# Layer-0 attention scores in four pieces of 260 columns, two to a pair of PSUM banks

## The chip, the cores and the metric

The kernel runs on one core of a Trainium2 chip. The metric is the device time of one execution in microseconds (us); the median of three runs stands for the kernel. TensorE (PE) multiplies and writes into PSUM, eight banks of 128 partitions x 512 float32 columns. VectorE (DVE), ScalarE (ACT) and GpSimd (POOL) work on 128 partitions at a time; DVE and ACT read PSUM, POOL works on SBUF alone here. Each engine takes its own instructions in order and waits on semaphores for the others.

## The reference

The program is an encoder trunk of two layers over 16 meta tokens and 1024 real ones, 1040 in all, with 1024 features. Each layer is `h + mixer(rmsnorm(h))` and then `h + mlp(rmsnorm(h))` with a squared ReLU; a final norm follows. The part that is changed is the mixer of layer 0, two groups of attention heads side by side:

```python
# A: 4 heads, each with two softmaxes over all 1040 keys
s = einsum('bqhcd,bshcd->bhcqs', q, k) * scale + bias      # c = 0, 1
p = softmax(s)
out_a = rmsnorm((p[c=0] - lam * p[c=1]) @ v) * (1 - lam_init)
# B: 8 query heads in two groups that share keys and values, no bias
out_b = softmax(einsum('bqkgd,bskd->bkgqs', q, k) * scale) @ v
h = h + concat(out_a, out_b) @ w_out
```

## The kernel before

Activations lie transposed, features on partitions and tokens along the free axis. A float32 product is made of passes over exact high and low parts.

The attention of layer 0 works on query tiles of 128 tokens. The unit of the first half of the work is a *job*: one query tile against one set of keys, which `scores` turns into the unnormalized probabilities of a [128, 1040] tile `sp` (`s` in the code). For A, head by head, a query tile has two jobs (c = 0, 1), and each head has one more small job for the 16 meta queries: 4 x (8 x 2 + 1) = 68 jobs. For B, `attend_b` takes two query tiles, each one job; with a small job for the meta queries of each group there are 66. That is 134 jobs.

`scores` cuts the 1040 keys into three chunks of 348, 346 and 346 columns (`CH_ALL`). For a chunk PE makes two matmuls (the high and the low part of the keys) into one PSUM bank of the ring "sc" (L500, L502). DVE takes the bank out into `s`, with the bias added in A (L504) or as it is in B (L507), and the same instruction accumulates the row minimum into a column of `mx`. After the three chunks DVE reduces the three columns to one (L514), and ACT makes the exponential of all 1040 columns in place and sums it (L516):

```python
mn = sm.tile([P, 2], F32, tag="mn", name=nm("mn"))
V.tensor_reduce(mn[:M, :n_], mx[:M, :n_], op=ALU.min, axis=AX.X)
A.activation(s[:M, :L], s[:M, :L], AF.Exp, bias=mn[:M, x:x + 1], scale=-1.0, accum_out=sums[:M, x:x + 1])
```

In A, POOL then combines the two probability tiles of a query tile (`head_a`: a scaling, L619, and an addition, L620; both over 1040 columns in SBUF); in B, POOL scales each by its inverse sum (`attend_b`, L673). The second half, `pv`, is a generator that is queued up to three groups behind (`AHEAD`): PE transposes the probabilities into a bank of the ring "tr" (L543), ACT takes out the high part `ph` (L557), DVE the low part `plo` (L559), and PE multiplies by the values into a bank of the ring "pv" (L572). At the end of a group ACT copies that bank out in A (L626); in B ACT copies half of it (L680) and DVE adds the other half to it (L686). After each head of A a norm follows: small DVE operations on [128, 9] tiles (`rsqrt_small`, L159 to L164; also L636).

PSUM is shared out by tags: `BANKS` gives the tags a, b, c two banks each and d, e one; `RINGS` says in which order a use goes around its tags: "sc" over c, c, d (three banks), "tr" over a, a, e (three), "pv" over b, b (two). One PSUM pool serves the whole kernel, so the projections before and the dense phases after use the same banks.

The program text sets what depends on what; a planner in the framework sets the order of the instructions on each engine, by its own cost figures, and places the semaphores.

Of the kernel before, what the change touches and what calls it, by code (L numbers as in the profile page):

```python
"""Two-layer encoder trunk (differential + axial GQA mixer, windowed GQA mixer, squared-ReLU MLPs).

Activations are held transposed, [feature, token], tokens in their own order (16 meta, 1024 real).
float32 products run as float32r passes over exact high/low parts of both operands.
"""
# [16 lines left out]
P = 128  # L22
L = 1040
# [23 lines left out]
BANKS = {"a": 2, "b": 2, "c": 2, "d": 1, "e": 1}  # L47
RINGS = {"proj": "ccde", "nat": "aa", "back": "bb", "sc": "ccd", "tr": "aae", "pv": "bb",
         "mm": "aaeccd", "st": "aaeccdbb", "sm": "bb", "pj1": "d", "pj1_first": "dcc", "sc1": "cc"}
WR = 2  # L50
# [24 lines left out]
def trunk(tc, hT, gT, w_in0, w_out0, w_up, w_down, w_in1, w_out1, rel, sinks, lamv, subln, qkn,  # L75
# [13 lines left out]
    def lay_out(pl, tags):  # L89
        """fix where a pool's slots lie: a first tile of each tag, in this order, handed to its first users."""  # L90
        kept = {}
        for tag, shape, dt, bufs in tags:
            kept[tag] = [pl.tile(shape, dt, tag=tag, bufs=bufs, name=nm(tag))]

        def get(tag, shape, dt, bufs):
            if kept.get(tag):
                return kept[tag].pop()
            return pl.tile(shape, dt, tag=tag, bufs=bufs, name=nm(tag))

        return get  # L100
# [6 lines left out]
    psU = pool("banks", space=PSUM)  # L107
    at, sqp = {}, []

    def bank(ring):  # L110
        i = at.get(ring, 0)
        at[ring] = i + 1
        tag = RINGS[ring][i % len(RINGS[ring])]
        return psU.tile([P, 512], F32, tag=tag, bufs=BANKS[tag], name=nm(ring))

# [22 lines left out]
    def load_w(src, lo_on=V, parts=1, to=None):  # L138
        """a [128, 8 x 128] tile of weights as the split halves of its columns."""
        raw = wp.tile([P, 1024], F32, tag="wr", bufs=WR, name=nm("wr"))  # L140
        for i in range(parts):
            c = slice(1024 // parts * i, 1024 // parts * (i + 1))
            D.dma_start(raw[:, c], src[:, c])
        return [split_w(raw[:, 512 * i:512 * i + 512], lo_on, to and to[i]) for i in range(2)]

    def mm3(ps, w, xh, xl, o, n, k0=0, k1=KT):
        """ps[:, :n] = the product over k from k0 to k1 (added to what is there if k0 > 0), columns o to o + n."""
        for k in range(k0, k1):
            wh, wl = w[k // 4]
            for i, (a, x) in enumerate(((wh, xh), (wh, xl), (wl, xh))):  # L150
                T.matmul(ps[:, :n], a[:, k % 4 * P:(k % 4 + 1) * P], x[k][:, o:o + n],  # L151
                         start=(k == 0 and i == 0), stop=(k == len(xh) - 1 and i == 2))

    def rsqrt_small(x, pw, n):
        """1/sqrt(x) of a [pw, n] tile by three Newton steps from the shifted-exponent guess."""
# [27 lines left out]
    def colsum(acc, c0, n, ps, scale, eps=None):  # L183
        """rows of mean(acc over partitions)+eps, one column for each token tile, then 1/sqrt."""
# [20 lines left out]
    def bcast_cols(y, tiles, newps, use):  # L205
        """use(psum, first column, width) gets y's entries laid along the free axis on every partition."""
# [10 lines left out]
    def make_r(acc, c0, n, smps, newps):  # L217
        """1/rms of the columns, over the sums of squares; acc may itself be wider."""
        y, tiles = colsum(acc, c0, n, smps, 1.0 / 1024)
        r = acc  # L220
        bcast_cols(y, tiles, newps, lambda ps, o, w: A.copy(r[:, o:o + w], ps[:, :w]))
        return r

# [41 lines left out]
    def project0(m, scale=None, w=None, raw=False, tags=()):  # L265
        """[128 columns of the projection, tokens] of the normed input; raw: without the norm's factor yet."""
# [15 lines left out]
    def spill_pair(i, parts):  # L282
        """high and low parts of [128, tokens] to DRAM; parts: [(source, first column, width)]."""
# [8 lines left out]
    def natural(z, use):  # L292
        """transposes of [128, tokens] by token tiles, four to a bank."""
# [16 lines left out]
    # axial rotary tables times the norm's gain  # L310
# [17 lines left out]
    def rope(z, tab, fscale, i_out):  # L328
        """normalize and rotate a pair of heads [2 x 64, tokens]."""
# [62 lines left out]
    # relative-position bias vectors, negated, to DRAM  # L392
# [5 lines left out]
    # each copied to 128 rows: read back with a row pitch shorter by one, row p is shifted by p  # L398
# [19 lines left out]
    # lambda  # L418
# [57 lines left out]
    def advance():  # L476
        """one piece of the oldest late work."""
# [9 lines left out]
    def beside(n, keep):  # L487
        """n pieces of late work, as long as more than keep works are waiting."""
# [4 lines left out]
    def scores(jobs, M, sums):  # L493
        """exp(q k + bias - row maximum) for each job, its row sums in the columns of sums.
        jobs: [([(q, k)], probabilities, bias)]; the products come out negated."""
        n_ = len(jobs)
        mx = sm.tile([P, 2, 3], F32, tag="mx", name=nm("mx"))
        for c, (o, n) in enumerate(CH_ALL):
            for x, (ops, s, bias) in enumerate(jobs):
                ps = bank("sc")  # L500
                for i, (q, k) in enumerate(ops):
                    T.matmul(ps[:M, :n], q, k[:, o:o + n], start=(i == 0), stop=(i == len(ops) - 1))  # L502
                if bias is not None:
                    V.tensor_tensor_reduce(out=s[:M, o:o + n], in0=ps[:M, :n], in1=bias[:M, o:o + n], scale=1.0,  # L504
                                           scalar=mx[:M, x, c - 1:c] if CHAIN and c else BIG, op0=ALU.add, op1=ALU.min, accum_out=mx[:M, x, c:c + 1])
                else:
                    V.tensor_scalar(s[:M, o:o + n], ps[:M, :n], 1.0, None, op0=ALU.mult, op1=ALU.min,  # L507
                                    accum_out=mx[:M, x, c:c + 1])
                beside(BESIDE, AHEAD - 1)
        if CHAIN and bias is not None:  # L510
            mn = mx[:, :, 2]
        else:
            mn = sm.tile([P, 2], F32, tag="mn", name=nm("mn"))
            V.tensor_reduce(mn[:M, :n_], mx[:M, :n_], op=ALU.min, axis=AX.X)  # L514
        for x, (_, s, _) in enumerate(jobs):
            A.activation(s[:M, :L], s[:M, :L], AF.Exp, bias=mn[:M, x:x + 1], scale=-1.0, accum_out=sums[:M, x:x + 1])  # L516
# [6 lines left out]
    def pv(ps_o, ptiles, vmats, passes, lo_pool=()):  # L523
        """ps_o[:, columns of the query tiles] = sum over keys; ptiles: [(probabilities, rows)]."""
# [10 lines left out]
        def split(r):  # L535
            run = runs[r]
            kw = TW[run[0]]
            pt = bank("tr")
# [41 lines left out]
    def head_a(h):  # L580
# [18 lines left out]
        for grp in GRPS:  # L599
            ptiles = []  # L600
            for t in grp:
# [13 lines left out]
                # p0 - lambda p1, each row times the sum of its first softmax: the norm after it takes that out  # L615
# [6 lines left out]
            def values(grp=grp, ptiles=ptiles):  # L622
                po = bank("pv")
# [7 lines left out]
        def norm_a():  # L631
# [5 lines left out]
            y, tiles = colsum(osq, 0, L, bank("tr"), 1.0 / 128, e0)  # L637
# [4 lines left out]
            def norm_b():  # L642
                yield
                bcast_cols(y, tiles, lambda: bank("tr"), fin)
# [17 lines left out]
    def attend_b(g, ptq, store):  # L662
# [12 lines left out]
        def values():  # L675
            po = bank("pv")
# [31 lines left out]
    run_late(0)  # L708
    pA.release()
    pE.release()  # L710
    if stop == "mix0":
# [6 lines left out]
        psU.release()  # L718
# [12 lines left out]
    def dense(layer, chunks, halves, sub, w_out, h_src, xp, yp, st, ht, by_pool, late_k,  # L731
              finish, done, last, spare=None, extra=None):
        """ht += mix w_out, then the feed-forward block added to ht.
        The feed-forward products run as seven half-size block products in place of eight (Winograd's form of
        Strassen's identity, over halves of k, rows and tokens); all of the hidden layer goes to DRAM between the
        two. The last 512 hidden features are taken directly, by groups of token chunks, their weights kept in tiles
        from spare() or loaded for each group."""
# [181 lines left out]
        # the pairs that the second products start with come last, and stay  # L919
# [15 lines left out]
        def after(n, e=0):  # L935
            """queue behind the n-th of the last part's additions (e=0) or sums of weights (e=1)."""
# [3 lines left out]
        def blocks(k, r1, r2, th, tl, n):  # L940
            """the seven token-side factors of tiles k of both halves of this part."""
# [149 lines left out]
    def split_q(src, q0, q1):  # L1091
        """[two heads x 64, n] to the stacks [high; low] and [low; high]."""
# [12 lines left out]
    def project1(w, z, o, n, ring, c, scale=1.0):  # L1105
        """columns o to o + n of a projection, to z from column c."""
# [15 lines left out]
    # keys: [meta, 0, 1, meta, 2, 3, meta, 4, 5, meta, 6, 7, meta] along the free axis  # L1122
# [160 lines left out]
    psU.release()  # L1283
# [24 lines left out]
def _layout(np, x, meta_tokens, rel_table, norm_attn, norm_mlp, norm_final, w_in_even, w_out_even, diff_lambda,  # L1308
# [4 lines left out]
    def second(w):  # L1313
        """by 512 rows: the four blocks of (tiles of rows in turn, halves of columns); the last 512 rows by pairs of column tiles."""
# [43 lines left out]
```

## Time and profile before

| | |
|---|---|
| median of three runs | 2626.34 us (2625.93 to 2629.81) |
| span of the profiled execution | 2630.9 us |
| share of the span busy: PE, DVE, ACT, POOL | 95%, 74%, 48%, 49% |
| scores of A, first to last | 254 to 465 us of the span |
| scores of B, first to last | 465 to 686 us |
| last products with the values of B | 725 us |

The profile records one execution. An instruction's row gives its start from the begin of the span and its duration; a duration includes waiting inside the instruction and the filling of the engine's pipeline, so the next row can start before the one ahead has ended. A busy share of PE counts such overlapped durations and does not mean that PE is at its peak. The idle time before an instruction is put down to the instruction that released it, as far as the semaphores show.

### The profile page before, as it was taken

How to read it: one execution, taken by the hardware profiler on the slowest of the kernel's cores; microseconds unless marked ns; L12 is line 12 of the kernel's file. 1: busy time of each engine (PE TensorE's matmuls, PEld its weight loads, DVE VectorE, ACT ScalarE, POOL GpSimd, SP SyncE). 2: the span in 40 equal slices, each digit the busy share in tenths (PEclk: the TensorE clock that was granted, in tenths of full speed). 3: DMA queues.
4: the chain of work that ended last, by engine and by line, in shares of the span. 5: the costliest groups of instructions: out<-in, count | busy, mean ns of one | idle time of the engine just before them, and what ended most of it. 6: DMA issues, size and time to landing. Idle time of an engine off the chain costs nothing. (4 is left out here: it accounts for less than half of the span.)

```text
span 2630.9 us, 42960 instructions
## 1 busy us (share of the span) xinstructions
PE 2508.9 (95%) x15440; PEld 2233.5 (85%) x15440; DVE 1937.8 (74%) x4057; ACT 1265.7 (48%) x2562; POOL 1281.2 (49%) x1214
## 2 busy tenths in 40 slices
PE   7999999999998999989999999999989999899997
PEld 7999888888898899988999988887868888676776
DVE  7834887798748566689898757777575656989975
ACT  3322656677634344453433547777344444443434
POOL 3300765333145223268877344556453223889854
PEclk9999999999998999999999999999989999999998
DMA  4378433200131532323232342232312332233322
GB/s 133 117 243 260 111 95 93 49 11 11 67 123 42 173 114 98 114 82 105 82 106 90 117 120 71 65 88 61 121 44 101 112 112 96 96 96 98 102 75 80
DMA packets 105494, 261.09 MB, mean 99 GB/s; under 512 B 16864, under 2 KB 48320, under 8 KB 104768
## 3 DMA queue, kind: packets, MB, share of 16 engines
q1 hardware_dynamic: 105280, 258.35, 30.9%
q8 instruction: 121, 1.98, 0.3%
q14 instruction: 93, 0.76, 0.1%
HBM read 191.40 MB, written 75.40 MB: 101 GB/s over the span
## 5 line engine op out<-in xcount | busy, mean ns | idle before, releaser
L854 PE MATMUL st<-h,wh 128*128 128x260 f32 (+1 forms) x2520 | 811.9, 326 | 45.3 <-DVE h L998 14.5
L854 PE MATMUL st<-l,wh 128*128 128x260 f32 (+1 forms) x2520 | 810.2, 324 | 6.6 <-DVE l L779 4.0
L854 PE MATMUL st<-h,wl 128*128 128x260 f32 (+1 forms) x2520 | 782.9, 325 | 14.8 <-DVE wl L135 8.8
L854 PEld LDWEIGHTS st<-h,wh 128*128 128x128 f32 x2520 | 480.3, 191 | 98.9 <-DVE h L998 19.9
L854 PEld LDWEIGHTS st<-h,wl 128*128 128x128 f32 x2520 | 474.4, 191 | 63.0 <-POOL wl L135 12.8
L854 PEld LDWEIGHTS st<-l,wh 128*128 128x128 f32 x2520 | 481.8, 191 | 45.0 <-DVE l L779 4.6
L134 ACT CAST wh<-wr 128x512 fp32r<-128x512 f32 x378 | 233.3, 619 | 408.7 <-PE st L854 228.7
L135 DVE TENSOR_TENSOR wl<-wr,wh 128x512 fp32r<-128x512 f32 x254 | 215.0, 848 | 178.9 <-ACT wh L134 178.3
L864 POOL TENSOR_TENSOR ws<-wr 128x512 f32<-128x512 f32 x32 | 43.2, 1350 | 412.7 <-DMA wr<-w_up 332.1
L135 POOL TENSOR_TENSOR wl<-wr,wh 128x512 fp32r<-128x512 f32 x124 | 177.0, 1430 | 67.0 <-ACT wh L134 62.2
L502 PE MATMUL sc<-stk,stk 128*128 128x346 f32 (+1 forms) x768 | 186.4, 356 | 8.1 <-DVE mx L504 7.9
L886 ACT ACTIVATE up<-up 128x260 f32<-128x260 f32 (+1 forms) x192 | 93.7, 491 | 193.2 <-DVE up L885 193.1
L516 ACT ACTIVATE sp<-sp,mn 128x1040 f32<-128x1040 f32 (+1 forms) x134 | 156.2, 1166 | 38.6 <-DVE mn L514 37.0
L998 DVE TENSOR_TENSOR h<-h,st 128x260 f32<-128x260 f32 x392 | 151.7, 417 | 29.7 <-PE st L854 27.3
L559 DVE TENSOR_TENSOR plo<-tr,ph 128x512 fp32r<-128x512 f32 (+3 forms) x260 | 153.4, 598 | 24.1 <-ACT ph L557 23.2
L557 ACT CAST ph<-tr 128x512 fp32r<-128x512 f32 (+3 forms) x260 | 130.3, 515 | 82.1 <-PE tr L543 56.5
L572 PE MATMUL pv<-ph,v 128*128 128x256 f32 (+3 forms) x594 | 157.3, 302 | 0.8 <-ACT ph L557 0.7
L998 DVE TENSOR_TENSOR hall<-hall,st 128x512 f32<-128x512 f32 x196 | 131.9, 681 | 31.2 <-PE st L854 28.7
L151 PE MATMUL mm<-l,wh 128*128 128x346 f32 (+3 forms) x440 | 150.9, 344 | 1.3 <-DVE l L762 1.2
L151 PE MATMUL mm<-h,wl 128*128 128x346 f32 (+3 forms) x440 | 150.1, 343 | 0.0
L151 PE MATMUL mm<-h,wh 128*128 128x346 f32 (+3 forms) x440 | 148.5, 344 | 1.2 <-ACT h L761 1.2
L673 POOL TENSOR_SCALAR sp<-sp,rsum 128x1040 f32<-128x1040 f32 (+1 forms) x66 | 74.2, 1138 | 152.5 <-DVE rsum L520 123.0
(273 smaller groups left out, 5943.0 us busy)
## 6 DMA issues: line engine op xcount, KB each, us to landing
wr<-w_down SPq DMA_DIRECT2D x68, 512.0 KB, 3.6
wr<-w_up SPq DMA_DIRECT2D x64, 512.0 KB, 3.5
stk<-stk_d SPq DMA_DIRECT2D x72, 260.0 KB, 7.0
sd<-up SPq DMA_DIRECT2D x28, 520.0 KB, 3.1
s<-sd SPq DMA_DIRECT2D x28, 520.0 KB, 3.1
sd<-up SPq DMA_DIRECT2D x28, 512.0 KB, 2.6
s<-sd SPq DMA_DIRECT2D x28, 512.0 KB, 3.5
wr<-w_in SPq DMA_DIRECT2D x27, 512.0 KB, 3.8
```

Of the source, the lines that this page charges most:

```text
L134: A.copy(h, src)
L135: lo_on.tensor_tensor(l, src, f32(h), op=ALU.subtract)
L151: T.matmul(ps[:, :n], a[:, k % 4 * P:(k % 4 + 1) * P], x[k][:, o:o + n], start=(k == 0 and i == 0), stop=(k == len(xh) - 1 and i == 2))
L502: T.matmul(ps[:M, :n], q, k[:, o:o + n], start=(i == 0), stop=(i == len(ops) - 1))
L516: A.activation(s[:M, :L], s[:M, :L], AF.Exp, bias=mn[:M, x:x + 1], scale=-1.0, accum_out=sums[:M, x:x + 1])
L557: A.copy(ph[:kw, :w], pt[:kw, :w])
L559: V.tensor_tensor(plo[:kw, :w], pt[:kw, :w], f32(ph[:kw, :w]), op=ALU.subtract)
L572: T.matmul(ps_o[:, :gw], vmats[v][:kw, j, :], (plo if lo else ph)[:kw, c], start=n_ == 0, stop=n_ == total - 1)
L673: G.tensor_scalar(s[:M], s[:M], rs[:M, i:i + 1], 1.0, op0=ALU.mult, op1=ALU.mult)
L854: T.matmul(acc_[x, o][:, :n], a[:, c], b[:, o:o + n], start=first and k == 0 and y == 0, stop=k == nk - 1 and y == 2, skip_group_check=not ...
L886: A.activation(r[:, c], r[:, c], AF.Square)
L998: marks[0].append(V.tensor_tensor(ht[m][:, c], ht[m][:, c], acc_[x, o][:, :n], op=ALU.add).ins)
```

## The change

The three chunks become four pieces of 260 columns. Two pieces lie in a pair of neighbouring banks (a tile of [128, 2, 512], columns 0 to 259 of each half), and DVE takes a pair out in one operation of 520 columns. `mx` has two columns in place of three, and the row minimum is made from the two by an elementwise minimum of two columns instead of a reduction. In the attention alone, a PSUM pool of its own holds two such pairs (tag "sc"), three banks for the transposes (tag "t", ring "tr0") and one for the products with the values (tag "o", ring "pv0"); the pool before is released ahead of it, and another is made after it for the dense phases. The rest of the diff takes out comments and the empty call of `beside`.

```diff
-RINGS = {"proj": "ccde", "nat": "aa", "back": "bb", "sc": "ccd", "tr": "aae", "pv": "bb",
+RINGS = {"proj": "ccde", "nat": "aa", "back": "bb", "tr": "aae", "pv": "bb", "tr0": "ttt", "pv0": "o",
+W_SC = 260
...
+    psU[0].release()
+    psU[0] = pool("banksA", space=PSUM)
...
-        n_ = len(jobs)
-        mx = sm.tile([P, 2, 3], F32, tag="mx", name=nm("mx"))
-        for c, (o, n) in enumerate(CH_ALL):
-            for x, (ops, s, bias) in enumerate(jobs):
-                ps = bank("sc")
-                for i, (q, k) in enumerate(ops):
-                    T.matmul(ps[:M, :n], q, k[:, o:o + n], start=(i == 0), stop=(i == len(ops) - 1))
...
+        for x, (ops, s, bias) in enumerate(jobs):
+            mx = sm.tile([P, 2], F32, tag="mx", name=nm("mx"))
+            for h in range(2):
+                sc2 = psU[0].tile([P, 2, 512], F32, tag="sc", bufs=2, name=nm("sc"))
+                for c in range(2):
+                    o = (2 * h + c) * W_SC
+                    for i, (q, k) in enumerate(ops):
+                        T.matmul(sc2[:M, c, 0:W_SC], q, k[:, o:o + W_SC], start=(i == 0), stop=(i == len(ops) - 1))
+                ps, out, mo = sc2[:M, :, 0:W_SC], halves(s, M, h), mx[:M, h:h + 1]
                 if bias is not None:
+                    V.tensor_tensor_reduce(out=out, in0=ps, in1=halves(bias, M, h), scale=1.0, scalar=BIG,
+                                           op0=ALU.add, op1=ALU.min, accum_out=mo)
                 else:
+                    V.tensor_scalar(out, ps, 1.0, None, op0=ALU.mult, op1=ALU.min, accum_out=mo)
-            mn = sm.tile([P, 2], F32, tag="mn", name=nm("mn"))
-            V.tensor_reduce(mn[:M, :n_], mx[:M, :n_], op=ALU.min, axis=AX.X)
+            mn = sm.tile([P, 1], F32, tag="mn", name=nm("mn"))
+            V.tensor_tensor(mn[:M], mx[:M, 0:1], mx[:M, 1:2], op=ALU.min)
+            A.activation(s[:M, :L], s[:M, :L], AF.Exp, bias=mn[:M], scale=-1.0, accum_out=sums[:M, x:x + 1])
+
+    def halves(t, M, h):
+        return t[:M, 520 * h:520 * h + 520].rearrange("p (a b) -> p a b", b=W_SC)
...
-            pt = bank("tr")
+            pt = bank("tr0")
...
-                po = bank("pv")
+                po = bank("pv0")
...
+    psU[0].release()
+    psU[0] = pool("banks1", space=PSUM)
```

## Rows read from the trace of the kernel before

**Rows 1.** A, B: busy us (instructions) of PE, PEld, DVE, ACT, POOL; clock, DMA.

```profile
254.00:465.00 211.00, 199.76 (x1276) 173.46 (x1275) 173.05 (x660) 131.19 (x257) 126.88 (x106) 0.96 0.40 108
465.00:690.00 225.00, 223.56 (x1555) 199.62 (x1553) 194.26 (x690) 164.27 (x317) 73.92 (x65) 0.98 0.10 27
```

**Rows 2.** Waits of DVE and ACT, 254 to 465 us: total, times, longest.

```profile
DVE sp L504 <- PE sc L502: 20.0, 34, 1.4
...
ACT sp L516 <- DVE mn L514: 24.0, 27, 4.9
```

**Rows 3.** DVE, start and duration, two take-outs in a row.

```profile
319.17 0.52 DVE L504 CUSTOM_DVE_ANT_0 sp<-sc,toe 128x346 f32<-128x346 f32 x1
...
319.61 0.52 DVE L504 CUSTOM_DVE_ANT_0 sp<-sc,toe 128x348 f32<-128x348 f32 x1
```

**Rows 4.** DVE groups of layer 1, one operation at two widths: busy, mean ns.

```profile
L1198 DVE CUSTOM_DVE_ANT_0 s<-sc,bt,nsink 128x400 f32<-128x400 f32 x96 | 59.1, 628 | 25.7 <-PE sc L1197 16.7 <-POOL s L1207 4.4 <-issue 2.6
L1198 DVE CUSTOM_DVE_ANT_0 s<-sc,bt,nsink 128x272 f32<-128x272 f32 x32 | 15.3, 495 | 6.2 <-PE sc L1197 5.6 <-issue 0.4
```

**Rows 5.** PE, start to start of matmuls of 346 and of 260 columns.

```profile
227.70 0.32 PE L151 MATMUL proj<-hg0h,wh 128*128 128x346 f32 x1
227.86 0.32 PE L151 MATMUL proj<-hg0l,wh 128*128 128x346 f32 x1
...
999.79 0.28 PE L854 MATMUL st<-h,wh 128*128 128x260 f32 x1
999.91 0.28 PE L854 MATMUL st<-l,wh 128*128 128x260 f32 x1
```

**Rows 6.** DVE and POOL side by side in A.

```profile
322.52 1.20 POOL L619 TENSOR_SCALAR sp<-sp,beta 128x1040 f32<-128x1040 f32 x1
...
323.15 0.60 DVE L162 TENSOR_TENSOR rst<-rsy 128x9 f32<-128x9 f32 x1
...
323.81 2.38 POOL L620 TENSOR_TENSOR sp<-sp,sp 128x1040 f32<-128x1040 f32 x1
...
324.11 0.14 DVE L514 TENSOR_REDUCE mn<-mx 128x1 f32<-128x3 f32 x1
324.17 2.05 DVE L163 SCALAR_TENSOR_TENSOR rst<-rst,cs 128x9 f32<-128x9 f32 x1
326.14 0.68 DVE L559 TENSOR_TENSOR plo<-tr,ph 128x512 fp32r<-128x512 f32 x1
```

**Rows 7.** Groups of DVE and POOL, 254 to 465 us: busy, mean ns.

```profile
L163 DVE SCALAR_TENSOR_TENSOR rst<-rst,cs 128x9 f32<-128x9 f32 x9 | 8.2, 908 | 0.1
L164 DVE SCALAR_TENSOR_TENSOR rsy<-rst,rsy 128x9 f32<-128x9 f32 x9 | 5.5, 606 | 0.1
L636 DVE SCALAR_TENSOR_TENSOR e<-es 128x8 f32<-128x8 f32 x4 | 4.4, 1111 | 0.0
L162 DVE TENSOR_TENSOR rst<-rsy 128x9 f32<-128x9 f32 x9 | 2.6, 291 | 0.1
...
L620 POOL TENSOR_TENSOR sp<-sp,sp 128x1040 f32<-128x1040 f32 x32 | 77.4, 2420 | 2.0
L619 POOL TENSOR_SCALAR sp<-sp,beta 128x1040 f32<-128x1040 f32 x32 | 38.8, 1211 | 68.9 <-DVE beta L617 30.6 <-DVE mn L514 23.6 <-PE sc L502 8.1
```

**Rows 8.** The same, 465 to 690 us.

```profile
L673 POOL TENSOR_SCALAR sp<-sp,rsum 128x1040 f32<-128x1040 f32 x62 | 69.8, 1138 | 141.7 <-DVE rsum L520 112.3 <-PE tr L543 13.5 <-DVE mn L514 12.2
...
L164 DVE SCALAR_TENSOR_TENSOR rsy<-rst,rsy 128x9 f32<-128x9 f32 x3 | 0.5, 161 | 0.0
```

**Rows 9.** End of one group of B and begin of the next, all engines.

```profile
541.47 0.38 PE L572 MATMUL pv<-plo,v 16*128 16x256 f32 x1
...
541.88 0.37 ACT L680 COPY ob<-pv 64x256 f32<-64x256 f32 x1 [0.16 <-PE pv L572]
...
542.62 0.40 DVE L686 TENSOR_TENSOR oc<-pv,ob 64x256 f32<-64x256 f32 x1
...
542.90 0.28 PE L572 MATMUL pv<-plo,v 128*128 128x256 f32 x1
```

More of the change, by code (lines that the diff above doesn't have):

```diff
@@ L46 @@
 CH_LAST = (16, 512), (528, 256), (784, 256)
-BANKS = {"a": 2, "b": 2, "c": 2, "d": 1, "e": 1}
-RINGS = {"proj": "ccde", "nat": "aa", "back": "bb", "sc": "ccd", "tr": "aae", "pv": "bb",
+BANKS = {"a": 2, "b": 2, "c": 2, "d": 1, "e": 1, "t": 3, "o": 1}
+RINGS = {"proj": "ccde", "nat": "aa", "back": "bb", "tr": "aae", "pv": "bb", "tr0": "ttt", "pv0": "o",
          "mm": "aaeccd", "st": "aaeccdbb", "sm": "bb", "pj1": "d", "pj1_first": "dcc", "sc1": "cc"}
+W_SC = 260
 WR = 2
@@ L106, in trunk @@
     tp = pool("temps", bufs=3)
-    psU = pool("banks", space=PSUM)
+    psU = [pool("banks", space=PSUM)]
     at, sqp = {}, []
@@ L113, in bank @@
         tag = RINGS[ring][i % len(RINGS[ring])]
-        return psU.tile([P, 512], F32, tag=tag, bufs=BANKS[tag], name=nm(ring))
+        return psU[0].tile([P, 512], F32, tag=tag, bufs=BANKS[tag], name=nm(ring))
     dr = top.enter_context(tc.tile_pool(name="dram", bufs=1, space=DRAM))
@@ L503, in scores @@
                 if bias is not None:
-                    V.tensor_tensor_reduce(out=s[:M, o:o + n], in0=ps[:M, :n], in1=bias[:M, o:o + n], scale=1.0,
-                                           scalar=mx[:M, x, c - 1:c] if CHAIN and c else BIG, op0=ALU.add, op1=ALU.min, accum_out=mx[:M, x, c:c + 1])
-                else:
-                    V.tensor_scalar(s[:M, o:o + n], ps[:M, :n], 1.0, None, op0=ALU.mult, op1=ALU.min,
-                                    accum_out=mx[:M, x, c:c + 1])
-                beside(BESIDE, AHEAD - 1)
@@ L510, in scores @@
-        if CHAIN and bias is not None:
-            mn = mx[:, :, 2]
-        else:
-            mn = sm.tile([P, 2], F32, tag="mn", name=nm("mn"))
-            V.tensor_reduce(mn[:M, :n_], mx[:M, :n_], op=ALU.min, axis=AX.X)
-        for x, (_, s, _) in enumerate(jobs):
-            A.activation(s[:M, :L], s[:M, :L], AF.Exp, bias=mn[:M, x:x + 1], scale=-1.0, accum_out=sums[:M, x:x + 1])
+                    V.tensor_tensor_reduce(out=out, in0=ps, in1=halves(bias, M, h), scale=1.0, scalar=BIG,
+                                           op0=ALU.add, op1=ALU.min, accum_out=mo)
+                else:
+                    V.tensor_scalar(out, ps, 1.0, None, op0=ALU.mult, op1=ALU.min, accum_out=mo)
@@ L636, in norm_a @@
             V.scalar_tensor_tensor(e0, es[:, :, 0], EPS, es[:, :, 0], op0=ALU.mult, op1=ALU.mult)
-            y, tiles = colsum(osq, 0, L, bank("tr"), 1.0 / 128, e0)
+            y, tiles = colsum(osq, 0, L, bank("tr0"), 1.0 / 128, e0)
             def fin(ps, o, w):
@@ L643, in norm_b @@
                 yield
-                bcast_cols(y, tiles, lambda: bank("tr"), fin)
+                bcast_cols(y, tiles, lambda: bank("tr0"), fin)
                 D.dma_start(mixd[0][h], oT)
@@ L675, in values @@
         def values():
-            po = bank("pv")
+            po = bank("pv0")
             yield from pv(po, ptiles, (vp[g],), ((0, 0), (0, 1)), LO_B)
@@ L717, in trunk @@
         tt.release()
-        psU.release()
+        psU[0].release()
         for p_ in (tp, sm, wp, cst): p_.release()
@@ L1282, in trunk @@
     yp.release()
-    psU.release()
+    psU[0].release()
     for p_ in (tp, sm, wp, cst):
```

## The prediction

> **What bounds the kernel now.** I read the page first for the place: the edit touches 254 to 690 us of a span of 2630.9 us, and every later phase needs the mixer's output, so what the two attention stretches gain or lose goes to the end. Next the busy times of those stretches [rows 1]. PE shows 200 of 211 us in A and 224 of 225 us in B, but its records overlap: a matmul of 346 columns lasts 0.32 us and the next starts after 0.16 us [rows 5], so these sums say little. DVE is the fullest engine whose records can be taken at their word: 173.05 of 211 us in A (82%), 194.26 of 225 us in B (86%). ACT has 62% and 73%, POOL 60% and 33%. Then the waits [rows 2]: in A, DVE waits 20.0 us for PE's scores and ACT 24.0 us for the row minimum. So the stretches are a chain of PE, DVE, ACT and POOL around few PSUM banks with DVE the nearest to full; its idle time is 211 - 173 = 38 us in A and 225 - 194 = 31 us in B. What is added to DVE costs, up to what this idle time takes up.
>
> **The take-out.** A chunk of 346 columns keeps DVE 0.44 us from start to start, its accumulator read included [rows 3]. For the width I take the slope of the same kind of operation in layer 1: (628 - 495) ns over 400 - 272 columns is 1.04 ns a column [rows 4]. A pair of 520 columns costs 0.44 + 174 x 0.00104 = 0.62 us. A job pays 3 x 0.44 = 1.32 us now and 2 x 0.62 = 1.24 us after: 0.08 us less, for 134 jobs **-10.7 us of DVE time**, 5.4 in A and 5.3 in B.
>
> **The matmuls.** A full job has six of about 346 columns at 0.16 us and gets eight of 260 at 0.12 us [rows 5]: 0.96 us both ways, with two more weight loads behind the matmuls, as they lie in the rows of 260. I take 0; the rounding of the rows (0.01 us between starts) leaves 0.1 us a job either way, 13 us of PE time in all, on an engine whose waits are no bound here.
>
> **The minimum.** L514 is a reduction of one SBUF tile. It becomes an elementwise minimum of two columns: two inputs, both in SBUF. The rows show that this is another class of operation while POOL works [rows 6]. L162 has two SBUF inputs; it starts at 323.15, lasts 0.60 us and ends at 323.75, just behind POOL's scaling (322.52 + 1.20 = 323.72). L163 starts at 324.17 and lasts 2.05 us, to 326.22; POOL's addition ends at 323.81 + 2.38 = 326.19. Between the two stands the reduction L514, begun at 324.11 within the same POOL instruction: 0.14 us. Behind L163 the next operation on DVE, L559, starts at 326.14: the whole queue stands. So a DVE operation with two SBUF inputs that meets a POOL instruction lasts until that one ends, however small it is; a reduction does not.
>
> How much it costs is bounded from two sides. By the operations that suffer today in A [rows 7]: L162, L163, L164 (9 each) and L636 (4) have means of 291, 908, 606 and 1111 ns, together (9 x 1805 + 4 x 1111) / 31 = 667 ns against 161 ns undisturbed [rows 8]: 0.51 us of waiting each. By an even spread of the minima over the stretch: POOL's 32 scalings of 1.21 us and 32 additions of 2.42 us hold it for a mean rest of half their length, so one minimum waits 32 x (1.21² + 2.42²) / 2 / 211 = 0.56 us. I take 0.5 us: 68 x 0.5 = **+34 us in A**. In B POOL has 62 scalings of 1.138 us [rows 8]: 62 x 1.138² / 2 / 225 = 0.18 us, for 66 minima **+11.8 us**. The lower bound is nothing, if the minima always fell between POOL's instructions; the upper one a hit for one of the two minima of every query tile of A with half of an addition and half a scaling (1.8 us), 58 us, and double the spread in B, 24 us.
>
> No row has a two-input DVE operation of one column beside POOL. The Trainium skill, SBUF — State Buffer, section Who interferes with whom, makes no exception for size: a DVE instruction with two SBUF inputs contends with a GpSimd instruction that reads SBUF, for the whole instruction, and a reduction never does. By that rule the +34 and +11.8 us stand; without it, if one column escaped, this part of the sum would be 0.
>
> Undisturbed, minimum and reduction cost the same (about 0.15 us, overlapped by the next row), so 0. Behind a blocked minimum stand the next take-outs, the low parts L559 and, on ACT, the exponential L516 that needs it; then PE, once both score pairs are full. POOL has slack.
>
> **The banks.** Scores get two slots of half a job for three of a third. Refilling one takes four matmuls, 4 x 0.12 + 0.16 = 0.64 us, while DVE takes 0.62 us for the other: even, and low parts fill the gap; I take 0, with 0.1 us x 268 = 27 us as the far end. Transposes keep three banks. The products with the values fall from two banks to one: the next group's first product must wait for ACT's copy and DVE's addition of the last. In one example [rows 9] the last product starts at 541.47, the addition ends at 543.02, and the next group's product came at 542.90: 0.12 us late, and at worst the whole 543.02 - 541.85 = 1.2 us. For the 34 groups of B I take 0.12 us, **+4 us**; the far end is 41 us. In A (16 groups) only a copy of the 0.37 us kind is in the way: 0. Handing the banks over at both ends of the attention I take as 0, as each slot waits for its own last user.
>
> **The sum.** DVE gets 34 + 11.8 - 10.7 = +35 us against 69 us of idle time. That idle time is no free room: it is made of waits for PE, which itself waits for the banks that DVE frees, so a late DVE is mostly a late loop; but some of it gives. I let two thirds through: +23.5, and with the bank +27.5 us. The profiled execution would be 2630.9 + 27.5 = 2658; it lies 4.6 us above the median of the runs, 2626.3, so the prediction is **2654 us**. About 0.2% (5.3 us) is what a measurement of this kernel can tell from no change.
>
> **The rivals.**
> Faster: the minima meet POOL seldom. POOL starts only after the second exponential of a query tile, so the loop could settle with the minima before and after POOL's stretch. Then the shorter take-outs remain, -10.7 us: 2616 us. It decides at a mean wait under 0.08 us per minimum (10.7 / 134). For it: the order on DVE is made anew, and POOL is idle 40% of A and 67% of B. Against it: POOL's 3.6 us per query tile run while DVE works on the next tile's two jobs. The Trainium skill, VectorE: DVE Perf Modes, section Rules for kernel authors, would have it so: fewer operations are what counts; a job has three in place of four. 13%.
>
> No change: waits as forecast, but DVE's 69 us of idle take them up: 35 us of which less than a sixth passes; 2621 to 2632 us. For it: PE's scores lie ready behind a blocked DVE. 11%.
>
> One bank for the values is the new wait: PE stands in order before the next group's first product while the scores behind it cannot be issued, 0.6 us x 34 = 20 us in B, with no lock worth naming: 2626 + 20 - 7 = 2639 us. For it: PE has one queue. Against it: DVE and ACT hold three transposed banks of work meanwhile. 6%.
>
> Both, at their far ends: 58 + 24 - 11 = 71 us in full and 4 or more from the bank, over 2690 us. 5%.
>
> The forecast has the other 65%, with 2632 to 2690 us as its own range.
>
> **How the numbers follow.** Faster by over 0.2%: 13%. Within 0.2%: 11%. Slower: 65 + 6 + 5 = 76%. The range leaves out the fast rival and the far end, 18%, and so runs from 2621 to 2690 us.
>
> **What would show it.** The take-outs: a group of 520 columns with a mean of 0.69 us, 268 of them, and 0.62 us from start to start. The minimum: its mean in A at 0.5 to 0.7 us, in B near 0.3, with single ones of up to 2.4 us that end with a POOL instruction; at 0.15 us throughout the forecast is wrong. Stretch A longer by some 20 us and B by some 8 us, with DVE's busy share at 85% or more in A. The bank: products with the values idle before a copy L680 or an addition L686. If A and B lengthen without long minima, the banks did it; if the minima are long and the stretches are not, the idle time took them up.

## The result and the profile after

The kernel after has a median of 2648.25 us (2645.77 to 2661.75, six runs) against 2629.71 us for the kernel before, measured beside it: 18.5 us slower, a ratio of 1.0070 (95% interval 1.0047 to 1.0093). That is clear of the 0.2% that can be told from no change, and lies inside the predicted range. The profiled execution took 2661.75 us with a span of 2660.0 us, 13.5 us above the median of its kernel, so its stages explain more than the 18.5 us.

The stretches of A and B first (columns as in [rows 1]). They are cut at this kernel's own times: A ends at 476 us, and B's stretch 6 us behind the last score (7 us in the kernel before):

```profile
254.00:476.00 222.00, 203.60 (x1419) 182.68 (x1417) 188.52 (x523) 131.57 (x257) 125.62 (x105) 0.94 0.38 101
476.00:705.00 229.00, 224.95 (x1675) 203.99 (x1674) 198.09 (x560) 169.62 (x317) 75.45 (x67) 0.96 0.10 26
```

A is 11 us longer and B 4 us. DVE's operations in A fell from 660 to 523 and its busy time rose from 173 to 189 us, 85% of the stretch. Line numbers are one or two higher than before: L163 to L165, L638 and POOL's L621 and L622 are L162 to L164, L636, L619 and L620 of the kernel before. The groups of DVE say where (254 to 475 us, then 475 to 705 us; busy, mean ns):

```profile
L509 DVE CUSTOM_DVE_ANT_0 sp<-sc,toe 128x520 f32<-128x520 f32 x128 | 86.2, 690 | 15.3 <-PE sc L506 14.2 <-issue 0.4 <-POOL toet L586 0.2
L514 DVE TENSOR_TENSOR mn<-mx 128x1 f32<-128x1 f32 x64 | 36.8, 575 | 0.3
...
L163 DVE TENSOR_TENSOR rst<-rsy 128x9 f32<-128x9 f32 x9 | 4.7, 521 | 0.1
L164 DVE SCALAR_TENSOR_TENSOR rst<-rst,cs 128x9 f32<-128x9 f32 x9 | 4.1, 453 | 0.0
L165 DVE SCALAR_TENSOR_TENSOR rsy<-rst,rsy 128x9 f32<-128x9 f32 x9 | 3.2, 356 | 0.1
L514 DVE TENSOR_TENSOR mn<-mx 48x1 f32<-48x1 f32 x4 | 1.4, 360 | 0.0
L638 DVE SCALAR_TENSOR_TENSOR e<-es 128x8 f32<-128x8 f32 x4 | 0.8, 188 | 0.0
...
L512 DVE TENSOR_SCALAR_CACHE_REDUCE sp<-sc 128x520 f32<-128x520 f32 x128 | 86.5, 694 | 7.5 <-PE sc L506 4.2
L514 DVE TENSOR_TENSOR mn<-mx 128x1 f32<-128x1 f32 x64 | 16.0, 250 | 0.2
```

The minimum, 145 ns before, has a mean of 575 ns in A and 250 ns in B. One of them beside POOL (start, duration):

```profile
262.49 1.21 POOL L621 TENSOR_SCALAR sp<-sp,beta 128x1040 f32<-128x1040 f32 x1 [1.72 <-DVE mn L514]
263.77 2.38 POOL L622 TENSOR_TENSOR sp<-sp,sp 128x1040 f32<-128x1040 f32 x1
...
263.70 0.08 DVE L509 DVE_READ_ACCUMULATOR2_ANT mx<- 128x1 f32 x1
263.82 2.36 DVE L514 TENSOR_TENSOR mn<-mx 128x1 f32<-128x1 f32 x1
266.10 0.69 DVE L509 CUSTOM_DVE_ANT_0 sp<-sc,toe 128x520 f32<-128x520 f32 x1
266.71 0.08 DVE L509 DVE_READ_ACCUMULATOR2_ANT mx<- 128x1 f32 x1
```

One column of one value per partition takes 2.36 us and ends at 266.18, 0.03 us behind POOL's addition (263.77 + 2.38 = 266.15); the next take-out starts only then. It is [rows 6] again, with the operation that the change put there. In the expectations below this is the "lock theory". The same view shows a take-out of 520 columns from 266.10 to the next row's 266.71: 0.61 us.

The second loss is at the other end, where the PSUM pool of the attention is closed and another opened (a pool boundary; the "bank theory" of the expectations). On PE, the last products with the values and the first of the output projection (`mm`):

```profile
736.37 0.38 PE L574 MATMUL pv<-ph,v 16*128 16x256 f32 x1
736.59 0.27 PE L574 MATMUL pv<-plo,v 16*128 16x256 f32 x1
736.79 0.43 PE L152 MATMUL mm<-h,wh 128*128 128x348 f32 x1
```

Before, the first `mm` ran at 689.5 us and 82 of them stood between the last products with the values, which ended at 725.1 us. After, none does. The busy times of the 20 us that begin 0.6 us behind the last score (at 699.4), and below them those of the same place in the kernel before (last score at 683.1):

```profile
700.00:720.00 20.00, 14.36 (x89) 11.60 (x88) 17.05 (x27) 14.69 (x25) 2.37 (x3) 0.92 0.48 170
...
684.00:704.00 20.00, 17.79 (x117) 15.61 (x117) 17.18 (x28) 15.12 (x24) 4.15 (x4) 1.00 0.52 193
```

PE has 14.4 of 20 us, at a mean granted clock of 0.92; before, it had 17.8 of 20 us at 1.00.

Times within the profiled executions (starts, in us of each span), for the kernel before, the one after and the experiments:

| kernel | A's last addition on POOL | last score | last product with values | first `mm` | first product of the MLP |
|---|---|---|---|---|---|
| before | 464.5 | 683.1 | 725.1 | 689.5 | 808.9 |
| after | 477.0 | 699.4 | 736.6 | 736.8 | 832.2 |
| reduction put back | 465.2 | 686.9 | 724.6 | 724.8 | 820.1 |
| before, two-input minimum | 476.5 | 700.0 | 742.6 | 706.9 | 826.5 |
| before, pool boundary at the end | 466.3 | 684.8 | 720.7 | 720.9 | 816.4 |
| before, pool boundary ahead of the attention | 464.0 | 683.9 | 726.3 | 690.6 | 810.2 |
| before, banks of after | 452.2 | 686.0 | 725.1 | 725.3 | 820.9 |
| after, pool closed earlier | 475.4 | 697.4 | 745.2 | 719.9 | 828.9 |
| two pools, reduction | 463.9 | 685.4 | 726.9 | 690.5 | 810.8 |
| two pools, elementwise minimum | 476.1 | 696.0 | 737.6 | 701.1 | 821.4 |
| before, norm on POOL | 460.0 | 685.7 | 726.9 | 691.4 | 810.6 |
| two pools, reduction, norm on POOL | 456.5 | 676.7 | 718.6 | 682.2 | 802.0 |

The kernels differ in two places. With a minimum of two SBUF inputs the last score comes at 696 to 700 us, without it at 683 to 687 (677 in the last row). From the last score to the first product of the MLP it takes 125 to 127 us where PSUM is not closed as a whole behind the attention, and 131 to 135 us where it is; there the first `mm` follows the last product with the values, but for the pool closed earlier.

### The profile page after: what moved, and what is told of

Same layout as the page of the kernel before. It is cut to its first block, busy times and chain, and to the rows that moved or that the text cites. A ratio compares the mean times of both kernels' runs of the same rounds, so it can differ in the third digit from the quotient of the medians.

```text
span 2660.0 us, 43326 instructions
## 1 busy us (share of the span) xinstructions
PE 2523.5 (95%) x15716; PEld 2255.3 (85%) x15716; DVE 1966.2 (74%) x3789; ACT 1267.7 (48%) x2562; POOL 1277.6 (48%) x1214
## 5 line engine op out<-in xcount | busy, mean ns | idle before, releaser
L136 DVE TENSOR_TENSOR wl<-wr,wh 128x512 fp32r<-128x512 f32 x254 | 208.9, 824 | 175.5 <-ACT wh L135 174.9
L506 PE MATMUL sc<-stk,stk 128*128 128x260 f32 x1024 | 181.5, 309 | 10.7 <-DVE mx L509 8.7
L506 PEld LDWEIGHTS sc<-stk,stk 128*128 128x128 f32 x1024 | 144.9, 200 | 18.2 <-DVE mx L509 11.8
```

Source lines behind the costliest of these rows:

```text
L136: lo_on.tensor_tensor(l, src, f32(h), op=ALU.subtract)
L506: T.matmul(sc2[:M, c, 0:W_SC], q, k[:, o:o + W_SC], start=(i == 0), stop=(i == len(ops) - 1))
```

## The experiments

Each ratio is to runs of the kernel before on the same chip; it is estimated from all runs, so it need not be the quotient of two medians.

### The reduction put back

```diff
-            V.tensor_tensor(mn[:M], mx[:M, 0:1], mx[:M, 1:2], op=ALU.min)
+            V.tensor_reduce(mn[:M], mx[:M], op=ALU.min, axis=AX.X)
```

> The kernel after, with the minimum of the two columns made by a reduction again (one SBUF input) in place of the elementwise minimum; all else as after. The lock theory (a two-input DVE operation lasts until POOL's instruction ends, and that is most of the loss): minima of 0.15 us throughout, 34 us of DVE waiting gone, two thirds of it off the time: some 18 to 23 us below the kernel after, that is within 5 us of the kernel before. The bank theory (the pool that ends behind the last product with the values keeps the output projection from starting, and that is most of the loss): the minima fall to 0.15 us all the same, but the time falls by 3 to 8 us only and stays 10 to 15 us above the kernel before.

Measured: 2639.19 us, 1.0029 (1.0016 to 1.0042). The order of the instructions is the same on every engine as in the kernel after; only the kind of these 134 differs. The minima and the norm's two-input operations in A, and the minima in B:

```profile
L514 DVE TENSOR_REDUCE mn<-mx 128x1 f32<-128x2 f32 x64 | 9.4, 147 | 0.3
L165 DVE SCALAR_TENSOR_TENSOR rsy<-rst,rsy 128x9 f32<-128x9 f32 x9 | 6.7, 740 | 0.1
L163 DVE TENSOR_TENSOR rst<-rsy 128x9 f32<-128x9 f32 x9 | 6.2, 688 | 0.1
...
L164 DVE SCALAR_TENSOR_TENSOR rst<-rst,cs 128x9 f32<-128x9 f32 x9 | 2.8, 315 | 0.0
L638 DVE SCALAR_TENSOR_TENSOR e<-es 128x8 f32<-128x8 f32 x4 | 2.2, 538 | 0.0
...
L514 DVE TENSOR_REDUCE mn<-mx 128x1 f32<-128x2 f32 x64 | 9.0, 140 | 0.2
```

The waits are gone, and with them 9 of the 18.5 us (11 us by the ratios). Neither theory's number: the minimum is about half of the loss, and 8 to 9 us remain. As the order is the same, the busy times from 254 us to the end of the last take-out can be set side by side, first with the reduction, then the kernel after:

```profile
254.00:689.60 435.60, 417.78 (x3085) 377.88 (x3084) 358.01 (x1079) 295.58 (x571) 201.18 (x171) 0.97 0.24 63
...
254.00:702.10 448.10, 425.87 (x3076) 384.78 (x3075) 384.44 (x1078) 298.30 (x570) 200.95 (x170) 0.95 0.23 61
```

With the elementwise minimum DVE is busy 26.4 us longer (384.4 for 358.0), idle 13.9 us less (63.7 for 77.6), and the stretch is 12.5 us longer.

### The two-input minimum alone

```diff
-            V.tensor_reduce(mn[:M, :n_], mx[:M, :n_], op=ALU.min, axis=AX.X)
+            V.scalar_tensor_tensor(mn[:M, 0:1], mx[:M, 0, 0:1], mx[:M, 0, 1:2], mx[:M, 0, 2:3], op0=ALU.min, op1=ALU.min)
```

> The kernel before, with its reduction of three columns replaced by one DVE operation with two SBUF inputs (and the third column as its scalar); banks and take-outs as before. The lock theory: minima with a mean near 0.6 us in A and 0.25 us in B, single ones of up to 2.4 us, and 15 to 30 us above the kernel before. The bank theory: the same long minima, but they disappear in DVE's idle time, and the time is within 6 us of the kernel before.

Measured: 2648.68 us, 1.0062 (1.0040 to 1.0084). The minima in A (two forms), then in B:

```profile
L514 DVE SCALAR_TENSOR_TENSOR mn<-mx 128x1 f32<-128x1 f32 x64 | 39.5, 617 | 0.2
...
L514 DVE SCALAR_TENSOR_TENSOR mn<-mx 48x1 f32<-48x1 f32 x4 | 3.9, 985 | 0.0
...
L514 DVE SCALAR_TENSOR_TENSOR mn<-mx 128x1 f32<-128x1 f32 x64 | 22.6, 353 | 0.1
```

One instruction per job, and nothing else of the change, makes the kernel before 0.6% slower, as the lock theory expected. But the planner also made the order anew: from 273 us on the engines' order is not that of the kernel before, so not all of the 16 us need be the waits.

### The pool boundary at the end alone

```diff
     run_late(0)
+    psU[0].release()
+    psU[0] = pool("banks1", space=PSUM)
```

> The kernel before, with its one PSUM pool closed behind the attention and a new one opened for the dense phases; tags, rings, scores and minimum as before. The bank theory: the first product of the output projection stands behind the last product with the values, PE has idle time at the tail, and the time is 8 to 13 us above the kernel before. The lock theory says nothing of this place: if the hand-over costs nothing, as the prediction took it, the time is within 3 us of the kernel before.

Measured: 2639.31 us, 1.0030 (1.0017 to 1.0044). PE at the boundary, and the busy times of 690 to 705 us and of two parts of them:

```profile
720.70 0.27 PE L572 MATMUL pv<-plo,v 16*128 16x256 f32 x1
720.90 0.43 PE L151 MATMUL mm<-h,wh 128*128 128x348 f32 x1
...
690.00:705.00 15.00, 11.18 (x50) 8.94 (x48) 13.43 (x17) 12.36 (x19) 2.24 (x2) 0.66 0.48 185
...
690.00:694.00 4.00, 1.10 (x7) 0.61 (x6) 2.43 (x5) 3.95 (x7) 1.26 (x2) 0.98 1.00 375
694.00:704.00 10.00, 9.07 (x37) 7.48 (x38) 10.00 (x12) 8.05 (x12) 0.98 (x1) 0.50 0.33 127
```

The kernel before, 690 to 705 us:

```profile
690.00:705.00 15.00, 13.50 (x86) 12.20 (x85) 14.00 (x18) 11.32 (x17) 2.24 (x2) 1.00 0.31 121
```

The same bank tags, opened anew, cost 0.30%. Up to 689.5 us, the first `mm` of the kernel before, the order on every engine is that of the kernel before; from there on PE has every `mm` behind the last product with the values, and the first one waits for nothing. The parts of the mixer's output that the first `mm` reads were written by 692.1 us:

```profile
689.77 1.06 ACT L763 CAST h<-l 128x1040 fp32r<-128x1040 f32 x1 [1.66 <-DMA l<-mixd]
...
690.86 1.24 DVE L764 TENSOR_TENSOR l<-l,h 128x1040 fp32r<-128x1040 f32 x1 [1.78 <-ACT h L763]
```

DVE had taken the last scores out of their banks by 687.5 us. So the data was there and the banks of the scores were free, and what held `mm` back to 720.9 us is its place in PE's order. That the planner puts it there because it gives a tile of the new pool its banks only once the old pool has handed over the last of its tiles is argued; the two pools below bear it out. PE loses the work that filled its gaps (11.2 of 15 us busy for 13.5), and its granted clock has a mean of 0.66 in this stretch.

### The boundary ahead of the attention alone

```diff
     # ---------- layer 0: attention ----------
+    psU[0].release()
+    psU[0] = pool("banksA", space=PSUM)
```

> The kernel before with its one PSUM pool closed ahead of the attention and opened anew, the mate of the boundary behind it; nothing else. If the boundary there holds the first scores back as the profiles of the kernels with it show (first scores at 256 to 258 us for 254): 2 to 4 us above the kernel before. The prediction's value: 0.

Measured: 2633.34 us, 1.0002 (0.9988 to 1.0017). The first score came at 256.4 us for 254.4, but the time does not show it. PE is busy with projections up to the boundary: all of 230 to 254 us in both kernels.

### The scores of before on the banks of after

```diff
+    psU[0].release()
+    psU[0] = pool("banksA", space=PSUM)
...
     run_late(0)
+    psU[0].release()
+    psU[0] = pool("banks1", space=PSUM)
```

In this pool "sc" goes around four banks (tag "s"), "tr0" around three ("t"), and "pv0" has one ("o").

> The scores of the kernel before (three chunks, each in a bank of its own, reduction of three columns) on the banks of the kernel after: a pool for the attention alone with four score banks, three for the transposes and one for the products with the values, closed and followed by a new one as after. If the one bank for the values costs the 4 us or more of the prediction on top of the hand-over: 2643 us or more. If the hand-over alone counts and bank shares and pairs are worth nothing: 2639 us, as with the pool boundary alone and as with the reduction put back.

Measured: 2641.01 us, 1.0031 (1.0019 to 1.0044): the boundary's 1.0030 and nothing more. The single bank for the values costs nothing that can be measured, and pairs or singles make no difference (1.0029 with pairs and the reduction). The intervals, 0.13% either way, do not by themselves rule out 4 us. The waits of PE and of its weight loads for DVE's addition `oc`, 254 to 735 us, are there but short, and the kernel before has none:

```profile
PE tr L545 <- DVE oc L688: 0.3, 1, 0.3
...
PEld pv L574 <- DVE oc L688: 1.6, 7, 0.2
```

In the kernel after they come to 1.4 us and 2.5 us.

### The pool closed earlier

```diff
-    run_late(0)
     psU[0].release()
     psU[0] = pool("banks1", space=PSUM)
+    own[0] = False
+    run_late(0)
```

With `own[0]` off, `bank` takes the rings "tr" and "pv" in place of "tr0" and "pv0".

> The kernel after, with the pool of the attention closed behind the last scores, ahead of the last three groups of transposes and products with the values, which take their banks from the pool of the dense phases (rings tr and pv as before); the elementwise minimum stays. The bank theory: the output projection runs between the last groups again, and the time falls by 8 to 13 us below the kernel after. The lock theory: by no more than 3 us.

Measured: 2648.62 us, 1.0062 (1.0041 to 1.0083), as the kernel after: a miss. The `mm` did run between the last groups, but from 719.9 us on, and the busy times of 700 to 720 us are those of the kernel after:

```profile
700.00:720.00 20.00, 14.38 (x86) 11.26 (x87) 15.63 (x24) 14.48 (x24) 2.25 (x2) 0.91 0.41 158
```

The last three groups have their banks from the new pool. But six groups are still to be multiplied by the values when the scores end (108 products): the other three (54) all run ahead of the first `mm`, so the gap stays where it was. From the last score to the first product of the MLP it takes 131.5 us, for 132.8 after and 125.8 before.

### Two pools, so that the score banks can be handed over by themselves

```diff
+    psU[:] = [None, pool("banksX", space=PSUM)]
+    psU[0] = pool("banksY", space=PSUM, side="right")
...
+    psU[0].release()
+    psU[0] = pool("banksZ", space=PSUM, side="right")
     run_late(0)
```

The first pool (t, t, t, o) stays open to the end; the second holds the score pairs and, closed behind the last scores, makes way for one of c, c, d, f. The rings become "tr": "ttt", "mm": "tttccd", "st": "tttccdof", "pv" and "sm": "of".

> The kernel after with the reduction, and with two PSUM pools from the attention on: one holds the three banks of the transposes and the one of the values and stays open to the end; the other holds the score pairs, is closed behind the last scores and followed by one of four banks for the dense phases, whose rings go around the same numbers of banks as before. So the output projection has banks while the last groups still run. Bank theory: the rest of the loss is the hand-over, so 2628 to 2633 us, the time of the kernel before, with products of the output projection between the last products with the values. Its rival, that the pairs or the single bank for the values cost what is left: 2638 us or more.

Measured: 2632.32 us, 0.9992 (0.9980 to 1.0003): no difference from the kernel before. On PE:

```profile
690.50 0.72 PE L153 MATMUL mm<-h,wh 128*128 128x348 f32 x3
...
692.00 0.38 PE L547 MATMUL tr<-ident,sp 128*16 128x128 f32 x2
692.14 0.37 PE L576 MATMUL pv<-ph,v 128*128 128x256 f32 x1
...
726.94 0.27 PE L576 MATMUL pv<-plo,v 16*128 16x256 f32 x1
```

The output projection starts at 690.5 us, between products with the values that go on to 726.9. With that and the reduction, all of the loss is gone, as the bank theory expected.

### Two pools with the elementwise minimum

> The kernel with two pools and the reduction, and the elementwise minimum of the kernel after put back in; the hand-over costs nothing here, so the minimum's wait stands by itself. By the difference of the kernel after and its copy with the reduction: 9 us above the two pools with the reduction, 2641 us. By the two-input minimum in the kernel before: 19 us above, 2651 us. Minima near 0.6 us in A and 0.25 us in B in both cases.

Measured: 2641.97 us, 1.0030 (1.0013 to 1.0048). The minima in A, then in B:

```profile
L516 DVE TENSOR_TENSOR mn<-mx 128x1 f32<-128x1 f32 x64 | 31.6, 494 | 0.3
...
L516 DVE TENSOR_TENSOR mn<-mx 128x1 f32<-128x1 f32 x64 | 16.0, 250 | 0.2
```

Minimum apart, this kernel has the order of instructions of the one with the reduction, but for one swap on DVE in layer 1. So the minimum alone is 1.0030 against 0.9992, 0.38% or 10 us (the intervals are 0.12% and 0.18% either way), and the boundary alone 0.30% or 8 us; together 0.68%, and the kernel after measured 0.70%.

### The norm's two-input operations on POOL

In the norm behind each head of A:

```diff
-            V.tensor_tensor(tv, yv, yv, op=ALU.mult)
-            V.scalar_tensor_tensor(tv, tv, -0.5, x, op0=ALU.mult, op1=ALU.mult)
-            V.scalar_tensor_tensor(yv, tv, 1.5, yv, op0=ALU.add, op1=ALU.mult)
+            G.tensor_tensor(tv, yv, yv, op=ALU.mult)
+            G.tensor_tensor(tv, tv, x, op=ALU.mult)
+            G.tensor_scalar(tv, tv, -0.5, 1.5, op0=ALU.mult, op1=ALU.add)
+            G.tensor_tensor(yv, tv, yv, op=ALU.mult)
...
-            V.scalar_tensor_tensor(e0, es[:, :, 0], EPS, es[:, :, 0], op0=ALU.mult, op1=ALU.mult)
+            G.tensor_tensor(e0, es[:, :, 0], es[:, :, 0], op=ALU.mult)
+            G.tensor_scalar(e0, e0, EPS, 1.0, op0=ALU.mult, op1=ALU.mult)
```

On the kernel before:

> The kernel before, with the two-input DVE operations of the norm behind each head of A (the three Newton steps and the squares of the sums, 10 a head) moved to POOL, as 14 small operations there; nothing else. Lock theory: the 17 us that these operations wait in A today go, a third to a half of it off the time: 2622 to 2626 us, unless POOL's own queue, some 3 us longer a head, gives it back. If DVE's idle time takes such waits up: 2629 to 2632 us.

Measured: 2636.32 us, 1.0006 (0.9992 to 1.0020): nothing. On the two pools with the reduction:

> Both of the last two edits on the kernel after with the reduction. If the theories hold and the edits add: 2620 to 2626 us, below the kernel before. If the longer take-outs leave DVE so free that the waits of the norm no longer count: as with the two pools alone.

Measured: 2626.37 us, 0.9972 (0.9958 to 0.9987) of the kernel before, here 2633.34 us. This version beats both kernels, by 0.28% and by about 1%. In A (254 to 465 us) DVE's busy time is 158 us of 211, for 173 before and 169 with the two pools alone:

```profile
254.00:465.00 211.00, 199.92 (x1433) 178.54 (x1432) 157.98 (x507) 134.25 (x264) 138.33 (x151) 0.97 0.44 114
```

Why the same edit gives nothing on the kernel before, whose DVE busy time in that stretch fell as far (157.5 us), is open: with the edit the planner's order differs from that of either kernel without it, and no run here holds it fixed. For the same reason the gain of 0.28% is that of the edit and the new order together.

## Why the prediction came out

The forecast, 2654 us and slower, was right in sign and within 6 us, and part of that is luck. It put the change at 27.5 us over 2626.3 us; measured are 18.5 us over 2629.7 us. Two terms, the minimum and the bank of the values, were 17 us too large together, and a term of 8 us was missing.

**The take-out** was right in its price: 690 and 694 ns a pair, 0.61 us from start to start for the 0.62 forecast, 268 of them. Its 10.7 us of DVE time is not seen at the end: with the rest of the loss removed the pairs stand at 0.9992 (0.9980 to 1.0003), so at most half of it got there.

**The minimum** was right in its mechanism, and its waits were a little over-sized. In A the minima have 36.8 + 1.4 = 38.2 us for 9.4 us and some 0.5 us of the four small ones as a reduction: 28 us of waiting for the 34 forecast. In B 16.0 against 9.0: 7 us for 11.8. What was wrong is the share that passes to the end. The term "I let two thirds through" made +23.5 us of 35 us net; measured, 35 us of waiting cost 9 us (the kernel after and the one with the reduction put back; 11 us by the ratios), and 30 us cost 10 us (two pools with either minimum): about 0.3. Both pairs have one order of instructions. In the first, the traces show where the rest went. Some of the waits only changed places: the norm's two-input operations and L638 have 6.7 + 6.2 + 2.8 + 2.2 = 17.9 us in A beside the reduction and 4.7 + 4.1 + 3.2 + 0.8 = 12.8 us after; that a minimum which waits first spares the operation behind it is the likely reason, and not shown. DVE's idle time took 13.9 of the 26.4 us that DVE was busy longer, and 12.5 us lengthened the stretch of these two executions. Against the kernel before, stretch A grew by 11 us for the "some 20" forecast and B by 4 for 8. On the kernel before a two-input minimum with 66 us in all, for about 25 us at its undisturbed 186 ns, cost 0.62% or 16 us: a share near 0.4, if all of it is the waits, as the order differs there.

The Trainium skill, SBUF — State Buffer, section Who interferes with whom, says that a DVE instruction with two SBUF inputs contends with a GpSimd instruction that reads SBUF, and that a reduction never does. The runs here agree: a one-column instruction with two SBUF inputs took up to 2.36 us beside a POOL instruction that reads SBUF, and reductions stayed at 0.12 to 0.16 us throughout.

**The banks.** "+4 us" for the single bank of the values was over-sized: its waits are there, 1.4 us of PE and 2.5 us of its weight loads in the kernel after, but no cost is seen, 1.0031 with it and 1.0030 without. "Handing the banks over at both ends of the attention I take as 0, as each slot waits for its own last user" is the step that failed. It holds at the begin (1.0002) and fails at the end: 0.30%, 8 us. The prediction thought of a slot's last user on the chip; what held the output projection back is its place in PE's order, behind the old pool's last products.

**The rivals.** The minima did meet POOL, so the faster one fell; more than half of their waiting did not reach the end, as the no-change rival said, but not five sixths; the bank of the values waits far less than the 20 us of its rival.

## What to carry to other kernels

A small DVE operation with two SBUF inputs is priced by the POOL instruction that it may meet, not by its columns. A reduction of the same columns avoids it (0.12 to 0.16 us), and so did the take-outs, whose one operand lies in PSUM: 0.67 to 0.70 us for 520 columns, all 128 of A, with POOL busy more than half of the time. A pool boundary orders work even where the chip has banks free: look in the trace at what ran across that place before, and hand over separately what comes free first. Where a forecast is made of waits on a nearly full engine, count how many of them replace other waits of the same kind, and leave the hand-overs a price of their own.

## What was not expected of the hardware

That one column is held as long as a whole tile (2.36 us) had no row in the kernel before. The gap at the tail also goes with a lower clock of TensorE. With the pool boundary at the end, PE was busy 1.1 of the 4 us from 690 to 694 us; from 694 to 704 us the granted clock was 0.50, its lower level of 1.2 GHz, with PE busy 9.1 of 10 us, and from 706 us on it was 1.00 again (2.4 GHz). In the kernel before it was 1.00 from 690 to 705 us, with PE busy 13.5 of 15 us.
